# Holding back the gated delta rule's steps until a step of the other recurrence has run

## The chip, the core and the metric

The kernel runs on one NeuronCore of one Trainium2 chip. The metric is the device time of one execution in microseconds, and the runs shown are compared by their median. The core has five engines with a queue each: TensorE (PE in the profile, its weight loads PEld), VectorE (DVE), ScalarE (ACT), GpSimd (POOL) and SyncE (SP), which here issues all DMAs. An engine works through its queue in order and waits on semaphores for what other engines produce.

## The reference

One layer of a streaming encoder, for a prompt of 2048 tokens and for a sample of 8 requests of 16 tokens, with model width 1024. One projection feeds two recurrences, the gated delta rule (GDN, 4 heads of 128) and RWKV-7 (8 heads of 64). Their outputs are projected back and a convolutional feed-forward of width 2816 follows.

```python
h = rms_norm(x, norm_mix); p = h @ w_in              # 1024 x 3880
q, k, v, z, beta, log_g = ...                        # short convolution, silu, l2 norm, gates
S_t = g_t (I - b_t k_t k_t^T) S_{t-1} + b_t k_t v_t^T;  o_t = S_t^T q_t            # GDN, by blocks
R_t = R_{t-1} diag(w_t) + (R_{t-1} a_t) b_t^T + v_t k_t^T;  y_t = R_t r_t          # RWKV-7
x += concat(norm(o) * silu(z), (norm(y) + bonus) * g) @ w_out
up = rms_norm(x, norm_ffn) @ w_up                    # 1024 x 5632
x += (silu(causal_dwconv(up[:2816])) * up[2816:]) @ w_down
y = rms_norm(x, norm_final)                          # and all end states
```

## The kernel before, in words

**Tiling.** Channels lie on partitions, tokens along the free axis. The 16 prompt blocks of 128 tokens are cut into five groups of 3, 4, 3, 3 and 3 blocks; the last group also takes the sample's 128 tokens. A group's tile is 384 or 512 tokens wide.

**Projections.** Every weight block of 128 x 512 is loaded by SP into `w32` (4 buffers), rounded by ACT to `whi`, and the remainder `wlo` is made by POOL and DVE in turn (4 buffers of each). TensorE multiplies three times (`whi` with both halves of the activations, `wlo` with the rounded half) in `mm3`, which yields after every two of the eight tiles, that is after six products. The products' results are `psi` (input projection), `pso` (output projection), `psga` and `psup` (up), `psd` (down), in a PSUM pool of four banks.

**Recurrences.** Both work on blocks of 128 tokens by the same plan: products of keys and queries, the inverse of a unit triangular matrix by doubled blocks (seven levels, each a step with `pR` and a step with `pX`, in 16-bit floats), then `pP` and `pC` for one Newton step, then outputs and the new state in 32-bit floats. GDN (`gdn_block`, names with a g: `TUg`, `Nhg`, `gkq`) does four heads at once, so one chain of steps per block: `pE`, `pG`, `pd`, `pk` (decays, transposed keys), `pKK`, `pF`, the inverse, `pw`, `po` and `pS`. RWKV-7 (`rwkv_half`, names with an r: `TUr`, `Nhr`, `rX`) does four of its eight heads at once, so two chains per block: `pA` and `pT` twice, `pZ`, the inverse, `pSA`, `pY` and `pSr`. For the sample, GDN reads and writes its states by request in the small steps `pKS` and `pSs`. All recurrence products share a second PSUM pool of four banks, which DVE and ACT empty. A block's last step (the tails, `pt` for GDN and `ptr` for RWKV-7) follows 8 us later.

**What sets the order.** Each part is a Python generator that yields how long, in nanoseconds, its next products' operands will take. `drive` (L389) keeps a clock of TensorE's work as `mm` and `tr` estimate it, and writes TensorE's instructions one step after the other: of the tasks whose time has come it takes the one of the lowest rank number, and when none is due a step of the projections, the main chain. The ranks are 0 for the small parts of a projection, 1 for tails, 2 for RWKV-7, 3 for GDN. A step waits `lat` after its predecessor, 2200 ns in an input phase and 2400 ns in an output phase, or what it yields itself. TensorE is the only engine under `manual_schedule`; the other queues are ordered by the framework around it. The phases are three input projections ahead and then output and input phases by turns; an output phase begins when both recurrences of its group are done.

Of the kernel before, what the change touches and what calls it, by code (L numbers as in the profile page):

```python
# [39 lines left out]
LATO = 2400  # L40
NEPS = 1e-6
# [25 lines left out]
C_F32 = C_SI        # float32 up to here, masks behind  # L67
# [39 lines left out]
def pack_host(a):  # L107
    """Layout only: slices, transposes, zero padding."""
# [79 lines left out]
class Group:  # L188
# [6 lines left out]
    def seg(self, t):  # L195
        """the sample's part of a [p, tokens] AP, by request"""
        return t[:, self.P:self.n].rearrange("p (s t) -> p s t", t=SEG)


def bc(a, n):  # L200
    """a, along a new last axis"""
    return a.unsqueeze(len(a.shape)).to_broadcast(list(a.shape) + [n])


class Build:
# [7 lines left out]
    # ------------------------------------------------------------ set-up  # L213
    def setup(self, ctx):
# [11 lines left out]
        # what the first products need, before all else  # L226
# [37 lines left out]
        # constants by value  # L264
# [3 lines left out]
        # parameters worked out once  # L268
# [8 lines left out]
        self.cw = der("cw", q("cw"), 0.5, own=True)           # half the taps: silu(y) = (1 + tanh(y/2)) y/2  # L277
# [7 lines left out]
        self.nea = q("alog")                        # -exp(a_log)  # L285
        nc.scalar.activation(self.nea, q("alog"), AF.Exp)
        nc.vector.tensor_scalar(self.nea, self.nea, -1.0, None, op0=MUL)
        # the scan's resets
# [7 lines left out]
        # conv histories, and the sample's  # L296
# [12 lines left out]
        # per-token and per-block scalars  # L309
# [7 lines left out]
        # states: minus GDN's, and RWKV's with keys on partitions  # L317
# [4 lines left out]
        self.SB = [cp.tile([128, 2, 2, 64], F32, name=f"SB{i}") for i in range(2)]      # by pairs of heads, block-diagonal  # L322
# [3 lines left out]
        # scratch  # L326
        for i, g in enumerate(self.groups):
            d = lambda n, s: self.dp.tile(s, F32, name=f"{n}{i}")
            g.gd = d("gd", [4, 4, 128, g.n])        # k q v z, by head
            g.rx = [d(f"rx{j}_", [5, 128, g.n]) for j in range(4)]  # L330
            g.rh = d("rh", [8, 128, g.n])
            g.l2 = [d(f"l2{j}_", [6, g.n]) for j in range(4)]
            g.og = d("og", [8, 128, g.n])

    # ------------------------------------------------------------ small helpers
# [3 lines left out]
    def a(self, g, name, dt=F32):  # L339
        """of the ring that the feed-forward's activations have in their phase"""  # L340
        return self.tp_.tile([128, 532], dt, tag="act", name=name, bufs=NACT)[:, 0:g.n]
# [31 lines left out]
    # ------------------------------------------------------------ the order of TensorE's work  # L373
    # Every part is a generator that yields how long (ns) its next products' operands take; the
    # products of the projections fill the time between those of the recurrences.
# [13 lines left out]
    def drive(self, main):  # L389
        """main to its end, then what is left of the tasks"""  # L390
        main = [0.0, 0, main]
        while main[2] is not None or self.tasks:
            ready = [t for t in self.tasks if t[0] <= self.clock]
            if ready:
                self.step(min(ready, key=lambda t: (t[1], t[0])))
            elif main[2] is not None and main[0] <= self.clock:
                self.step(main)
            else:
                self.clock = min([t[0] for t in self.tasks] + ([main[0]] if main[2] is not None else []))
# [9 lines left out]
    def load_w(self, src, tiles=KT):  # L409
        """[128, tiles * 128] of a weight, by [128, 512]"""  # L410
# [8 lines left out]
    def split_w(self, src, tiles=KT, ws=None):  # L419
        """a weight as pairs of [128, 512]: rounded, and what is left"""  # L420
# [12 lines left out]
    def mm3(self, ps, w, xs):  # L433
        """ps = sum over tiles of w^T x, both split: three passes"""
# [10 lines left out]
    def load_tok(self, g, t, a):  # L445
        """a group's tokens from [128, all tokens] of DRAM"""
# [25 lines left out]
    def rms(self, g, acc):  # L472
        """in place: 1/rms of the channels whose squares acc sums by partition, on every partition"""
# [11 lines left out]
    def rsqrt(self, out, ps, scale=1.0):  # L485
        """(scale ps + eps)^-1/2"""
# [6 lines left out]
    def split_x(self, g, x, w=None):  # L493
        """x, times w of each channel: rounded, and what is left"""
# [10 lines left out]
    # ------------------------------------------------------------ causal convolution of a projected tile  # L505
    def conv(self, g, ps, rs, taps, hist, samp, out, rows=128):
        """out = conv of ps rs over the tokens; hist and samp become the last rows"""
# [28 lines left out]
    # ------------------------------------------------------------ input projection and all that is per token  # L536
    def phase_in(self, g):
# [17 lines left out]
        # low-rank inputs  # L555
# [29 lines left out]
    def gates(self, g, P, S):  # L585
        """beta and log decay of each token and GDN head, tokens on partitions"""
# [16 lines left out]
        # -beta = -(1 + tanh(b/2))/2  # L603
        nc.scalar.activation(w[0], ba[:, :, 0:4], AF.Tanh, scale=0.5)
        nc.vector.tensor_scalar(self.nbeta[:, sl], w[0], -0.5, -0.5, op0=MUL, op1=ADD)
        # log_g = -exp(a_log) (max(u,0) + ln(1 + exp(-|u|)))
# [9 lines left out]
    def l2scale(self, g, j, qk, kk):  # L616
        """(sum of squares over a head's channels + eps)^-1/2 of RWKV's keys, GDN's queries and keys: the sums
        side by side in the array, 32 rows each, and the results spread over the partitions through DRAM"""
# [47 lines left out]
    def prep_rwkv(self, g, j, block, la, sga, sgb, qk):  # L666
# [7 lines left out]
        # decay  # L674
# [12 lines left out]
        def pc(t):              # a tile's prompt tokens, by chunks  # L687
# [10 lines left out]
        # a chunk's exponents from its middle, the sample's from its start  # L698
# [16 lines left out]
        # learning rate a = (1 + th)/2  # L715
# [15 lines left out]
        def rest():  # L731
# [6 lines left out]
            # k (1 + (a - 1) k_a)  # L738
# [6 lines left out]
            # bonus and gate  # L745
# [14 lines left out]
            # the keys' direction  # L760
# [7 lines left out]
            # -kk a exp(-L)  # L768
# [8 lines left out]
    # ------------------------------------------------------------ inverse of four unit upper triangular matrices  # L777
    def inverse(self, N, levels, x):
        """(I - N)^-1 of N [128, 4, 128] (rows before columns): doubled blocks, then one Newton step"""
# [9 lines left out]
        for lv in range(levels):  # L789
# [3 lines left out]
            def v(t, o):        # [.., nb, b] of 128 columns: the first or the second of each pair of blocks  # L793
# [10 lines left out]
            if lv == 0:         # both from the identity, in which the products are plain  # L804
# [35 lines left out]
    # ------------------------------------------------------------ gated delta rule, a block of 128 tokens, four heads  # L840
    def gdn_block(self, g, i, samp=False):
# [11 lines left out]
        # decays  # L853
# [39 lines left out]
        # products of keys, queries with keys  # L893
# [11 lines left out]
        # through the state  # L905
# [50 lines left out]
        # norm over the head, gate  # L956
# [40 lines left out]
    # ------------------------------------------------------------ RWKV-7, a block of 128 tokens, four of the heads  # L997
    def rwkv_half(self, g, i, hf, samp=False):
# [21 lines left out]
        for p in range(2):  # L1020
            x = X[p]
            pA = [self.psr("pA").rearrange("p (n t) -> p n t", n=2) for e in range(2)]
            for n in range(2):
                for e in range(2):      # the halves of the array at once
# [49 lines left out]
        # outputs  # L1074
# [6 lines left out]
        # norm over the head, gate  # L1081
# [12 lines left out]
        # state  # L1094
# [59 lines left out]
    def rec(self, part):  # L1154
        """a recurrence through all groups, each once it is prepared"""
# [7 lines left out]
    # ------------------------------------------------------------ output projection and feed-forward  # L1163
# [75 lines left out]
    def finish(self, g, res, rs):  # L1239
        """the last norm"""  # L1240
# [34 lines left out]
def order(n):  # L1275
    """of the phases: three input projections ahead, then by turns"""
# [37 lines left out]
```

## Time and profile before

| | |
|---|---|
| median of 3 runs | 3566.49 us (3560.24 to 3572.14) |
| profiled execution, its span; the page gives no other time of it | 3558.0 us |
| TensorE busy | 3372.0 us, 95% |
| VectorE, GpSimd, ScalarE busy | 2376.5 us, 1833.0 us, 1510.7 us |
| mean granted TensorE clock | 0.972 |
| TensorE's weight loads busy | 2895.7 us |

The profiled execution's span is 8.5 us below the median of the runs and 2.2 us below the fastest. In a timeline row the first number is when the instruction, or the merged row, began, the second how long it lasted; rows of TensorE overlap, since its matmuls are pipelined, so what a product costs is the distance from its beginning to the next one's. A bracket gives the idle time of the engine before the row and who ended it. "L360" is the line of the helper `mm` that issues every product, so rows are told apart by their tiles.

### The profile page before, as it was taken

The page shows a single profiled execution, that of the slowest core. Times are in us where ns is not written, and L with a number is a line of the kernel's source. Part 1 is how long each engine was busy: PE and PEld are TensorE (multiplying, and loading weights), DVE is VectorE, ACT ScalarE, POOL GpSimd, SP SyncE. Part 2 cuts the span into 40 slices and gives each one's busy share as a digit, 9 for nine tenths or more (in the row PEclk, how much of TensorE's full clock was granted, in tenths as well). Part 3 has the DMA queues.
Part 4 walks back from the last instruction along what each step waited for, and adds up shares of the span by engine and source line. Part 5 has one row for each costly group of instructions (what it writes and reads, how often), then busy time and mean ns, then how long its engine had stood idle before and what let it go on. Part 6 is the DMA issues. An engine that isn't in the chain of part 4 may idle for free. (4 is left out here: it accounts for less than half of the span.)

```text
span 3558.0 us, 60074 instructions
## 1 busy us (share of the span) xinstructions
PE 3372.0 (95%) x21661; PEld 2895.7 (81%) x21661; DVE 2376.5 (67%) x4277; ACT 1510.7 (42%) x2698; POOL 1833.0 (52%) x2335
## 2 busy tenths in 40 slices
PE   8989989999999989999999999899999999999997
PEld 7867768788999977777777767799979899988886
DVE  7777777786776677666655677776566665665444
ACT  5554344444333455443333455443324434453333
POOL 4545545655664544455454445566555355534442
PEclk9989999999999999999999999999999999999999
DMA  5534444453333344532222334533343433443322
GB/s 174 167 130 131 140 150 128 139 167 107 110 108 114 123 140 143 169 97 86 92 92 92 112 136 143 191 112 112 112 140 121 159 123 129 137 139 97 97 94 81
DMA packets 346265, 447.58 MB, mean 126 GB/s; under 512 B 30168, under 2 KB 194336, under 8 KB 345968
## 3 DMA queue, kind: packets, MB, share of 16 engines
q1 hardware_dynamic: 345968, 443.75, 38.9%
q8 instruction: 170, 2.79, 0.3%
q14 instruction: 127, 1.04, 0.1%
HBM read 372.60 MB, written 71.03 MB: 125 GB/s over the span
## 5 line engine op out<-in xcount | busy, mean ns | idle before, releaser
L425 ACT CAST whi<-w 128x512 fp32r<-128x512 f32 (+1 forms) x1070 | 651.2, 610 | 1115.7 <-PE psd L360 295.5
L429 POOL TENSOR_TENSOR wlo<-w,whi 128x512 fp32r<-128x512 f32 (+1 forms) x535 | 706.9, 1321 | 676.3 <-ACT whi L425 625.2
L360 PE MATMUL psi<-x,whi 128*128 128x384 f32 (+1 forms) x2480 | 737.7, 378 | 33.8 <-ACT x L501 14.0
L360 PEld LDWEIGHTS psi<-x,whi 128*128 128x128 f32 x2480 | 456.4, 196 | 96.2 <-issue 23.9
L360 PE MATMUL psup<-x,whi 128*128 128x384 f32 (+1 forms) x1760 | 504.3, 367 | 0.0
L360 PE MATMUL psga<-x,whi 128*128 128x384 f32 (+1 forms) x1760 | 502.6, 366 | 0.0
L429 DVE TENSOR_TENSOR wlo<-w,whi 128x512 fp32r<-128x512 f32 (+1 forms) x535 | 426.2, 797 | 77.0 <-ACT whi L425 76.8
L360 PE MATMUL psi<-x,wlo 128*128 128x384 f32 (+1 forms) x1240 | 456.2, 368 | 3.2 <-POOL wlo L429 3.1
L360 PEld LDWEIGHTS psga<-x,whi 128*128 128x128 f32 x1760 | 315.5, 189 | 28.1 <-issue 3.3
L360 PEld LDWEIGHTS psup<-x,whi 128*128 128x128 f32 x1760 | 316.4, 190 | 25.7 <-issue 1.8
L360 PE MATMUL psd<-ah,whi 128*128 128x384 f32 (+1 forms) x880 | 330.2, 375 | 7.0 <-ACT ah L1213 7.0
L360 PE MATMUL psd<-al,whi 128*128 128x384 f32 (+1 forms) x880 | 319.7, 363 | 4.5 <-POOL al L1215 4.5
L360 PE MATMUL psd<-ah,wlo 128*128 128x384 f32 (+1 forms) x880 | 318.7, 362 | 0.0
L360 PE MATMUL psup<-x,wlo 128*128 128x384 f32 (+1 forms) x880 | 316.6, 360 | 0.0
L360 PE MATMUL psga<-x,wlo 128*128 128x384 f32 (+1 forms) x880 | 315.3, 358 | 0.0
L1223 DVE TENSOR_TENSOR res<-res,psd 128x384 f32<-128x384 f32 (+1 forms) x240 | 145.3, 605 | 212.8 <-PE psd L360 212.1
L360 PEld LDWEIGHTS psi<-x,wlo 128*128 128x128 f32 x1240 | 241.7, 195 | 26.3 <-POOL wlo L429 5.0
L1215 POOL TENSOR_TENSOR al<-xin,ah 128x384 fp32r<-128x384 f32 (+1 forms) x110 | 126.0, 1146 | 144.4 <-ACT ah L1213 100.7
L513 DVE TENSOR_TENSOR P<-psga,rsx 128x384 f32<-128x384 f32 (+1 forms) x110 | 64.2, 584 | 197.7 <-PE psga L360 192.5
L360 PE MATMUL pso<-x,whi 128*128 128x384 f32 (+1 forms) x640 | 187.5, 373 | 8.9 <-DVE x L499 7.4
L360 PEld LDWEIGHTS psd<-ah,whi 128*128 128x128 f32 x880 | 167.3, 190 | 23.9 <-ACT ah L1213 8.5
L821 DVE TENSOR_TENSOR TUr<-TUr,pX 128x256 f16<-128x256 f16 x396 | 148.5, 412 | 53.2 <-PE pX L360 51.7
(342 smaller groups left out, 6753.4 us busy)
## 6 DMA issues: line engine op xcount, KB each, us to landing
w<-in_w_up SPq DMA_DIRECT2D x440, 256.0 KB
w<-in_w_in SPq DMA_DIRECT2D x310, 256.0 KB
w<-in_w_down SPq DMA_DIRECT2D x160, 256.0 KB
rX<-rx SPq DMA_DIRECT2D x68, 320.0 KB
w<-in_w_out SPq DMA_DIRECT2D x80, 256.0 KB
w<-in_w_down SPq DMA_DIRECT2D x80, 192.0 KB
rx<-res SPq DMA_DIRECT2D x48, 192.0 KB
gd<-res SPq DMA_DIRECT2D x48, 192.0 KB
```

Of the source, the lines that this page charges most:

```text
L360: self.nc.tensor.matmul(out, lhsT=lhsT, rhs=rhs, start=start, stop=stop)
L425: nc.scalar.copy(hi, w)
L429: eng.tensor_tensor(lo, w, hi.bitcast(F32), SUB)
L513: nc.vector.tensor_tensor(P[:, h:h + g.P], ps[:, 0:g.P], rs[:, 0:g.P], MUL)
L821: nc.vector.tensor_tensor(w, w, pX[:, y].rearrange("p u (n b) -> p u n b", b=b), ADD)
L1215: nc.gpsimd.tensor_tensor(lo, y, hi.bitcast(F32), SUB)
L1223: nc.vector.tensor_tensor(res[m], res[m], ps, ADD)
```

## The change

`drive` holds a GDN step back. When a projection step could go and nothing but projection work has run since the last one (`joined` is false), tasks of rank 3 are left out of the choice, unless they have been due for `PATIENCE`, 3500 ns of the driver's clock. As soon as another task has put products in (a step of RWKV-7, a tail, a small part), `joined` becomes true and the GDN step that is due follows at once, ahead of the next projection step. Where no projection step can go, nothing is held back. The last branch now looks only at tasks whose time lies ahead. The rest of the diff takes out comments, which moves line numbers by one to eight.

```diff
+PATIENCE = 3500
...
     def drive(self, main):
         main = [0.0, 0, main]
+        joined = False
         while main[2] is not None or self.tasks:
             ready = [t for t in self.tasks if t[0] <= self.clock]
+            go = main[2] is not None and main[0] <= self.clock
+            if go and not joined:
+                ready = [t for t in ready if t[1] < 3 or t[0] + PATIENCE <= self.clock]
             if ready:
+                at = self.clock
                 self.step(min(ready, key=lambda t: (t[1], t[0])))
-            elif main[2] is not None and main[0] <= self.clock:
+                joined = joined or self.clock > at
+            elif go:
+                joined = False
                 self.step(main)
             else:
-                self.clock = min([t[0] for t in self.tasks] + ([main[0]] if main[2] is not None else []))
+                self.clock = min([t[0] for t in self.tasks if t[0] > self.clock] + ([main[0]] if main[2] is not None else []))
```

The instructions are the same in number and kind on every engine. Three places on TensorE show the move.

A step of GDN's inverse in the third group's output phase (`Nhg`, `TUg` are GDN's, `Nhr`, `TUr` RWKV-7's; `psga` and `psd` are projections). Before, a step alone:

```order
L360 MATMUL psga<-x,whi 128x384 x2
L360 MATMUL psga<-x,wlo 128x384
L360 LDWEIGHTS Nhg
L360 MATMUL pR<-TUg,Nhg 128x64
...
L360 MATMUL psga<-x,whi 128x384 x2
L360 MATMUL psga<-x,wlo 128x384
```

The same step with the change:

```order
L361 LDWEIGHTS nid_122
L361 MATMUL pP<-TUr,nid_122 128x128
L361 LDWEIGHTS Nhg
L361 MATMUL pR<-TUg,Nhg 128x64
...
L361 MATMUL psd<-ah,whi 128x384
L361 MATMUL psd<-al,whi 128x384
```

It stood between two projection steps; now it stands behind RWKV-7's `pP` step, with no projection product between the two. In the whole program TensorE leaves the projections 718 times before and 618 times with the change; of the 100 joints gained, 71 are between 16-bit steps of the two inverses.

The sample's state steps of GDN. Before, two of them with one projection step between:

```order
L360 MATMUL pSs<-gwm,gkt 128x512
L360 MATMUL psga<-x,whi 128x384 x2
L360 MATMUL psga<-x,wlo 128x384
L360 MATMUL psga<-x,whi 128x384 x2
L360 MATMUL psga<-x,wlo 128x384
L360 MATMUL pSs<-gwm,gkt 128x512
```

With the change, two of them in the same part:

```order
L361 MATMUL pR<-TUr,Nhr 128x64
L361 MATMUL pSs<-gwm,gkt 128x512
L361 MATMUL psd<-ah,whi 128x384
...
L361 MATMUL psga<-x,whi 128x384 x2
L361 MATMUL psga<-x,wlo 128x384
...
L361 MATMUL pR<-TUr,Nhr 128x64
L361 MATMUL pSs<-gwm,gkt 128x512
```

Each now follows a step of RWKV-7, and twelve projection products lie between the two where six lay.

The head of a GDN block in the third input phase. Before:

```order
L360 MATMUL pE<-lm,gtr 128x512 x2
L360 MATMUL pG<-lm,onr 128x512 x2
L360 MATMUL pd<-lg,con 128x4
L370 MATMUL pk<-con,gkq 128x128 x4
L360 LDWEIGHTS Nhr
L360 MATMUL pR<-TUr,Nhr 128x64
...
L360 MATMUL psi<-x,whi 128x384 x2
L360 MATMUL psi<-x,wlo 128x384
L370 MATMUL pt<-con,gon 128x128 x4
L360 MATMUL pKK<-gkq 128x256 x4
```

With the change:

```order
L361 MATMUL pE<-lm,gtr 128x512 x2
L361 MATMUL pG<-lm,onr 128x512 x2
L361 MATMUL pd<-lg,con 128x4
L371 MATMUL pk<-con,gkq 128x128 x4
L371 MATMUL pt<-con,gon 128x128 x4
L361 MATMUL pKK<-gkq 128x256 x4
L361 LDWEIGHTS TUr
L361 MATMUL pX<-Rr,TUr 128x64
```

The head's six tiles and the tail now come in one stretch, with no projection product inside it. Stretches that fill more than six banks before a projection product comes are 20 before and 32 with the change.

## The prediction

> **What bounds the kernel now.** I read the page first, then TensorE's waits, then its timeline at places where a recurrence step stands between projections.
>
> ```profile
> span 3558.0 us, 60074 instructions
> PE 3372.0 (95%) x21661; PEld 2895.7 (81%) x21661; DVE 2376.5 (67%) x4277; ACT 1510.7 (42%) x2698; POOL 1833.0 (52%) x2335
> PEclk9989999999999999999999999999999999999999
> ```
>
> TensorE bounds the whole span: 95% busy, the next engine 67%. So time can go in three ways only: TensorE's products take less each, it waits less (it is idle for 3558.0 - 3372.0 = 186.0 us), or its clock is granted more often. The third is in the view of cores:
>
> ```profile
> core 0: 3558.0 us, clock 0.972
> ```
>
> At a mean of 0.972 about 3558.0 x 0.028 = 100 us of the span went to a lower clock (an estimate, as if all of it were products). The waits, longest in total first, with their number and the longest one:
>
> ```profile
> PE pG L360 <- DVE rA L1027: 11.3, 2, 5.7
> PE pA L360 <- DVE rA L1027: 8.9, 5, 3.6
> PE pSs L360 <- DVE gwm L970: 7.3, 5, 2.9
> PE pR L360 <- DVE TUg L821: 3.3, 2, 2.7
> PE pKS L360 <- DMA gS<-in_st_gdn: 2.5, 1, 2.5
> PE pA L360 <- DVE SN L984: 2.1, 3, 0.7
> PE pX L360 <- DVE Rg L803: 1.6, 3, 0.7
> PE pE L360 <- POOL lm L857: 1.5, 2, 0.9
> PE pA L360 <- DVE gkt L890: 1.3, 1, 1.3
> ```
>
> The reader is to see two kinds. In five rows a GDN step waits for its own operands (`pSs` for `gwm`, `pR` for `TUg`, `pKS` for its state, `pX` for `Rg`, `pE` for `lm`): 7.3 + 3.3 + 2.5 + 1.6 + 1.5 = 16.2 us. In the other four, `pG` and `pA` wait for something that isn't their operand: DVE has not emptied the PSUM bank they want (11.3 + 8.9 + 2.1 + 1.3 = 23.6 us). The first kind shrinks when GDN comes later, the second can grow when recurrence steps stand closer.
>
> **The returns to the projections.** What a step costs beyond its products shows in TensorE's timeline. First a GDN step alone, as before the change; then one of the places where, already before, a GDN step happens to follow an RWKV-7 step of the same kind:
>
> ```profile
> 2387.41 0.51 PE L360 MATMUL psga<-x,whi 128*128 128x384 f32 x2
> 2387.76 0.34 PE L360 MATMUL psga<-x,wlo 128*128 128x384 f32 x1
> 2387.93 0.30 PE L360 MATMUL pR<-TUg,Nhg 128*128 128x64 f16 x4
> 2388.07 0.60 PE L360 MATMUL psga<-x,whi 128*128 128x384 f32 x2
> 2388.50 0.34 PE L360 MATMUL psga<-x,wlo 128*128 128x384 f32 x1
> ```
>
> ```profile
> 2402.44 0.33 PE L360 MATMUL psd<-ah,wlo 128*128 128x384 f32 x1
> 2402.61 0.29 PE L360 MATMUL pR<-TUr,Nhr 128*128 128x64 f16 x4
> 2402.74 0.28 PE L360 MATMUL pR<-TUg,Nhg 128*128 128x64 f16 x4
> 2402.85 0.42 PE L360 MATMUL psd<-ah,whi 128*128 128x384 f32 x1
> 2403.11 0.34 PE L360 MATMUL psd<-al,whi 128*128 128x384 f32 x1
> 2403.29 0.33 PE L360 MATMUL psd<-ah,wlo 128*128 128x384 f32 x1
> ```
>
> A projection product costs 0.175 us from beginning to beginning (2387.41 to 2387.76 for two). From 2387.76 to 2388.50 lie three products, 0.52 us, and the step: it costs 0.74 - 0.52 = 0.22 us. From 2402.44 to 2403.11 lie two products, 0.35 us, and two steps, which together cost 0.67 - 0.35 = 0.32 us. Apart they would cost 0.44. The saving is about 0.10 us a joint, with the rows' rounding 0.085 to 0.12; most of it is the first product behind a recurrence step, which takes 0.26 us (2402.85 to 2403.11) in place of 0.175.
>
> The order has 100 joints more. For the 71 between 16-bit steps I take the row: 71 x 0.10 = 7.1 us. For the other 29 a 32-bit step joins in, for which I quote no row of this kind; it can save nothing (the 32-bit step may pay the same start inside the stretch) or the same 0.10, and I take the middle, 29 x 0.05 = 1.5 us. The sum is **8.6 us**, with bounds 71 x 0.085 = 6.0 and 100 x 0.12 = 12.
>
> **GDN's own waits.** Held back, a step finds its operands more often. For `pSs` the order gives one more projection step, six products of 0.175 us or 1.05 us, between two of them. Five waits shortened by up to 1.05 us each are 5.2 us of the 7.3; the eight waits of the other four rows lose their whole length or 1.05 us each, 3.3 us to 1.65 for `TUg`, about 1.6 in `Rg`, 1.5 in `lm`, 1.05 in `pKS`: up to 5.8. Not all of it comes, since a step that starts later also makes its successor's operands later, and `PATIENCE` is counted on the driver's clock, which is not TensorE's own. I take half of the 11.0, rounded down: **5 us**; bounds 0 and 16.2.
>
> A held step also issues its DMAs later: a block's loads of `gkq` and `gV` with its first step, `gz` with `pw`, `gS` with `pKS` and `pSs`. They move with the step whose successors need them. SP's queue is not what they would hold up:
>
> ```profile
> SPq L415 <- POOL wlo L429: 1182.0, 450, 8.1
> SPq L415 <- DVE wlo L429: 714.6, 403, 7.0
> ```
>
> SP stands 1896.6 us waiting for a free weight buffer, so weights are loaded as early as buffers allow, and a GDN load that is issued a step later changes nothing ahead of it. I cost it at nothing; if a load came late it would appear as another row like that of `pKS`, 2.5 us.
>
> **PSUM banks.** Four banks serve both recurrences. What a bank wait looks like where a GDN head follows an RWKV-7 `pA`:
>
> ```profile
> 2286.89 1.28 DVE L1027 TENSOR_TENSOR rA<-pA,msk 128x512 f32<-128x512 f32 x2
> 2287.63 1.22 PE L360 MATMUL pG<-lm,onr 128*128 128x512 f32 x2 [5.56 <-DVE rA L1027]
> ```
>
> DVE needs 1.28 us for the two `rA`, but TensorE stood 5.56 us, because DVE came to them late. The change makes some of these places better (GDN's head no longer stands where it stood) and makes 12 more stretches of over six banks. On the one side, the two `pG` waits go, with 11.3 us, less what replaces them (I allow 3): -8 us. On the other, each of the 12 longer stretches waits for two evictions, 12 x 1.28 = +15 us. I take **0**, since the row stands for two places out of 17 heads, and keep both ends.
>
> **The clock.** It drops behind long waits:
>
> ```profile
> 2544.15 0.34 PE L360 MATMUL psga<-x,wlo 128*128 128x384 f32 x1
> 2547.04 1.05 PE L360 MATMUL pKS<-gkqs,gS 128*128 128x32 f32 x8 [2.55 <-DMA gS<-in_st_gdn]
> 2548.04 0.59 PE L360 MATMUL psga<-x,whi 128*128 128x384 f32 x2
> 2552.03 0.52 PE L360 MATMUL psup<-x,wlo 128*128 128x384 f32 x1
> ```
>
> After 2.55 us without a product the same product shows 0.52 us in place of 0.34. Over the kernel, 100 us lost to the clock stand beside 186.0 us of idle time, 0.54 for each. For the 5 us of waits saved that is **2.7 us**. The Trainium skill, in "TensorE: Matmul & The Clock Gate", section "HAM oscillation — how this bites in real kernels", has the clock fall to half when an idle gap crosses a window of about 3.4 us, and not in proportion to all idle time. By that rule short waits that shrink bring back no clock at all and the sum would be 2.7 us less. The row above agrees as to its kind, with a gap of 2.55 us.
>
> **The sum.** 8.6 + 5 + 0 + 2.7 = 16.3 us, from 3558.0 to about 3542 us of span. The median shown lies 8.5 us over the span; I carry that along: 3566.5 - 16.3 = 3550 us. All favourable bounds together are 12 + 16.2 + 8 + 0.54 x 24.2 = 49 us; all unfavourable, 15 + 0.54 x 15 - 6.0 = 17 us slower.
>
> **Rivals.** *Only the returns.* Waits move rather than vanish: the waits that a later GDN step avoids come back at RWKV-7's `pA`, which now finds GDN's tiles ahead of it. Then 8.6 us are left: 3558 us, which counts as no change. For it speaks that GDN's own waits are only 16.2 of 186.0 us of idle time; against it, that RWKV-7 keeps the first place whenever both are due.
>
> *The banks turn the sign.* In the head shown in the order, `pE`, `pG`, `pd`, `pk`, `pt`, `pKK` and RWKV-7's `pX` come with no projection product between. If each of the 12 added stretches waits for the 1.28 us of two evictions and GDN's own waits don't shrink, that is 15.4 us, and 0.54 of it again from the clock, 23.7 in all; less 8.6 from the returns it is 15 us slower, 3582 us. It decides from 8.6 / (12 x 1.54) = 0.47 us a stretch. For it speak the 23.6 us of bank waits; against it, that 20 such stretches already stand in the program and only the few rows above came of them. The Trainium skill, in "Perfetto Trace Analysis", section "Optimizing Tensor Performance", asks that independent groups of matmuls rotate through banks so that emptying one overlaps with the next group's products; this change takes away the projection products that did that here.
>
> *GDN becomes the last.* If it fell behind RWKV-7, an output phase would wait for it.
>
> ```profile
> L360 PE MATMUL pS<-gw,gkt x128: 274/275/276, 299.7 to 2525.3; 128*128 128x128 f32 x128
> L360 PE MATMUL pSr<-rSA,rtok x256: 221/222/271, 290.1 to 2759.1; 128*64 128x64 f32 x128
> ```
>
> GDN's last prompt block ends 234 us ahead of RWKV-7's. A block has some 22 steps; at 3.5 us each the last group's three blocks and its sample lose 308 us, 74 too many: 3640 us. But that needs every step held to the limit, though RWKV-7 has a step about every 3 us.
>
> **How the numbers follow.** I give the forecast 0.53, only the returns 0.26, the banks 0.19, the late GDN 0.02. What counts as a change is 0.3%, 10.7 us, about what a measurement of this kernel can tell. The first case is faster, the second the same (with a hundredth more for cases near the bound), the others slower with a hundredth off: 0.53, 0.27, 0.20. The range reaches down by 38 us, not the full 49, since all favourable bounds will hardly meet, and up to the bank rival: 3528 to 3581 us. The likeliest case alone spans 3536 to 3556.
>
> **What would show it.** Right: more places where `pR<-TUg` follows `pR<-TUr` or `pX` without a projection product; the waits `pSs <- gwm`, `pR <- TUg` and `pX <- Rg` smaller in sum than 13; a mean clock of 0.972 or a little more. The return's price is wrong if the joined steps cost 0.44 together. The bank term is wrong if waits of `pG`, `pA`, `pKK` or `pX` for a DVE row that isn't their operand sum to well over 23.6 us. The whole is wrong if idle time grows, which would mean that waits on DVE, busiest in the input phases, follow another pattern than the rows quoted here.

## The result, and the profile after

| | before | with the change |
|---|---|---|
| median of 12 runs each | 3563.24 us (3559.36 to 3572.14) | 3543.36 us (3532.66 to 3562.39) |
| ratio | | 0.9947, 95% interval 0.9935 to 0.9959 |
| profiled execution: its own time; its span | not given; 3558.0 us | 3551.17 us; 3549.3 us |
| mean granted TensorE clock, median of the runs | 0.973 | 0.977 |

The change is faster by 19.9 us, 0.53%; by the interval 15 to 23 us. The forecast was 16.3 us faster. The sign and the size came as predicted. The terms did not all hold, and most of what follows is about that.

The page and the cores view of the changed kernel, to be held against the first rows of the prediction:

```profile
span 3549.3 us, 60010 instructions
PE 3360.1 (95%) x21661; PEld 2893.1 (82%) x21661; DVE 2396.0 (68%) x4277; ACT 1512.3 (43%) x2698; POOL 1837.8 (52%) x2335
```

```profile
core 0: 3549.3 us, clock 0.975
```

TensorE is busy for 3372.0 - 3360.1 = 11.9 us less, and idle for 189.2 us, not 186.0: this pair shows no gain in waits. Two cautions belong to these numbers. The profiled execution of the change lies above the median of its runs (3551 against 3543), so it shows 8.7 us of the 20. The profile before was one of the faster runs: a run of the change takes 1.9 us longer than its span, and the prediction carried 8.5. And two profiles of the kernel before differ by 6 us in TensorE's busy time (3372.0 and 3365.8) and 9 us in its idle time (186.0 and 194.7), so differences of that size in one pair prove nothing.

The waits of TensorE in the changed kernel (total us, number, longest), first GDN's own and the banks, then three rows of RWKV-7:

```profile
PE pSs L361 <- DVE gwm L978: 6.9, 2, 4.5
PE pX L361 <- DVE Rg L811: 6.0, 3, 4.6
PE pR L361 <- DVE TUg L814: 2.6, 3, 1.1
PE pR L361 <- DVE TUg L829: 2.4, 4, 1.2
PE pE L361 <- POOL lm L865: 0.4, 1, 0.4
PE pA L361 <- DVE rA L1035: 23.1, 11, 5.4
PE pA L361 <- DVE gkt L898: 0.9, 1, 0.9
...
PE pX L361 <- DVE Rr L811: 14.2, 11, 4.6
PE pR L361 <- DVE TUr L829: 11.6, 10, 3.6
PE pZ L361 <- DVE rA L1035: 1.4, 3, 1.1
```

The rows of RWKV-7 that answer to these in the kernel before, which the prediction did not show:

```profile
PE pZ L360 <- DVE rA L1027: 8.0, 3, 4.1
PE pR L360 <- DVE TUr L806: 6.1, 2, 5.9
PE pX L360 <- DVE Rr L803: 5.6, 5, 3.9
PE pR L360 <- DVE TUr L821: 4.3, 6, 1.2
```

The reader is to see that waits changed place. The two `pG` waits on `rA` (11.3 us) and the `pKS` wait on its state (2.5) are gone. But `pA` on `rA` went from 8.9 to 23.1, `pX` on `Rr` from 5.6 to 14.2, and `pR` on `TUr` from 10.4 to 12.1 (11.6 and, by the same view, 0.5 at L814); `pZ` on `rA` fell from 8.0 to 1.4. Summed over all rows of the two views, the waits in front of GDN's steps fell from 38.6 to 24.1 us, and those in front of RWKV-7's rose from 63.6 to 78.8.

The joined step, in the timeline, behind `pP` where the order showed it:

```profile
2407.45 0.22 PE L361 MATMUL pP<-TUr,nid 128*128 128x128 f16 x1
2407.50 0.28 PE L361 MATMUL pR<-TUg,Nhg 128*128 128x64 f16 x4
2407.62 0.42 PE L361 MATMUL psd<-ah,whi 128*128 128x384 f32 x1
2407.88 0.34 PE L361 MATMUL psd<-al,whi 128*128 128x384 f32 x1
```

`pR` takes 0.12 us to the next product, and the 0.26 us of the first projection product is paid once for both steps: the price that the prediction read from the kernel before. It is no matter of one place: in the profile before, the first 384-wide projection product behind a 16-bit step took 0.259 us in the median of 326 places at full clock, one behind another projection product 0.174. Two long stretches show that one without a projection product can go with or without a wait. A head in an output phase, seven tiles and no wait:

```profile
2392.77 0.29 PE L361 MATMUL pR<-TUr,Nhr 128*128 128x64 f16 x4
2392.90 0.70 PE L361 MATMUL pE<-lm,gtr 128*128 128x512 f32 x2
...
2394.95 1.89 PE L361 MATMUL pKK<-gkq 128*128 128x256 f32 x8
2396.68 0.28 PE L361 MATMUL pX<-Rr,TUr 128*128 128x64 f16 x4
```

And a stretch where an input phase ends and an output phase begins:

```profile
770.54 0.29 PE L361 MATMUL pR<-TUg,Nhg 128*128 128x64 f16 x4
770.76 1.13 PE L361 MATMUL pA<-rX 64*128 64x256 f32 x8
...
777.00 0.37 PE L361 MATMUL pX<-Rg,TUg 128*128 128x64 f16 x4 [4.62 <-DVE Rg L811]
779.61 2.07 PE L361 MATMUL pA<-rX 64*128 64x256 f32 x6 [0.88 <-DVE rA L1035]
782.95 0.52 PE L361 MATMUL pso<-x,wlo 128*128 128x384 f32 x1
```

Here GDN's `pX` holds everything for 4.62 us, though its `pR` had been through 6 us before, because DVE made `Rg` late; then `pA` waits for a bank, and the projection behind shows 0.52 us instead of 0.34. This need not be a price of the change: near the same change of phase the kernel before stands too, 4.07 us at `pZ` for `rA`.

### The profile page after: what moved, and what is told of

Its sections match the earlier page's. It is cut to its first block, busy times and chain, and to the rows that moved or that the text cites. A ratio compares the mean times of both kernels' runs of the same rounds, so it can differ in the third digit from the quotient of the medians.

```text
span 3549.3 us, 60010 instructions
## 1 busy us (share of the span) xinstructions
PE 3360.1 (95%) x21661; PEld 2893.1 (82%) x21661; DVE 2396.0 (68%) x4277; ACT 1512.3 (43%) x2698; POOL 1837.8 (52%) x2335
## 5 line engine op out<-in xcount | busy, mean ns | idle before, releaser
L437 DVE TENSOR_TENSOR wlo<-w,whi 128x512 fp32r<-128x512 f32 (+1 forms) x535 | 435.3, 814 | 77.0 <-ACT whi L433 76.1
```

What stands on the lines that cost most here:

```text
L437: eng.tensor_tensor(lo, w, hi.bitcast(F32), SUB)
```

## The experiments

Three properties of an order can be told apart: how late a GDN step goes after it is due (its mean in the driver's own order), how often TensorE leaves the projections ("returns", counted in the order), and which steps meet which work of DVE. The theories on trial are those of the prediction (the returns; GDN's own waits; the banks; the clock) and, from the second kernel on, a rival: that a later GDN step is what helps, joined or not.

| kernel | returns | GDN late by, us | median us | ratio to before, 95% | median clock |
|---|---|---|---|---|---|
| before, again | 718 | 1.10 | 3563.36 | 1.0000 (0.9987 to 1.0012) | 0.973 |
| the change | 618 | 1.46 | 3543.36 | 0.9947 (0.9935 to 0.9959) | 0.977 |
| held, never joined | 925 | 1.59 | 3564.11 | 0.9998 (0.9986 to 1.0011) | 0.9755 |
| joined early, not held | 638 | 0.73 | 3603.52 | 1.0118 (1.0099 to 1.0138) | 0.9665 |
| held, and joined early | 619 | 1.08 | 3552.99 | 0.9980 (0.9964 to 0.9995) | 0.9755 |
| later, not joined | 737 | 1.35 | 3542.58 | 0.9944 (0.9923 to 0.9965) | 0.978 |
| inverse steps only | 630 | 1.32 | 3560.50 | 0.9993 (0.9976 to 1.0009) | 0.972 |
| other steps only | 683 | 1.18 | 3554.43 | 0.9977 (0.9962 to 0.9993) | 0.976 |
| the change, both recurrences later | 643 | | 3537.91 | 0.9930 (0.9910 to 0.9951) | 0.977 |
| another order (parts) | 717 | 1.02 | 3563.87 | 1.0002 (0.9993 to 1.0012) | 0.976 |
| another order (tails) | 717 | 1.10 | 3555.71 | 0.9981 (0.9972 to 0.9990) | 0.975 |
| sample steps only | 709 | 1.16 | 3557.44 | 0.9982 (0.9970 to 0.9994) | 0.974 |
| the change, GDN later | 626 | 1.96 | 3556.93 | 0.9977 (0.9968 to 0.9986) | 0.974 |

(Lateness counts the 400 ns where an experiment adds them; it is left out where both recurrences were moved.)

**The kernel before again**, unchanged, as a measure of what a comparison can tell.

> The kernel before, unchanged, for the span and the granted clock of each of its runs. Theory 'clock': its clock lies near 0.970 to 0.972 where the changed kernel's twelve runs had 0.972 to 0.981 with a median of 0.977, and over the runs of both kernels span falls by about 3.3 us for each 0.001 of clock, so that at one and the same clock the two kernels differ by less than 5 us. Theory 'returns': the clocks of both kernels are alike, and at one clock the changed kernel is 8 us or more faster.

Measured: 3563.36 us beside 3563.66, ratio 1.0000 within 0.0012. A difference of 5 us between two kernels is visible here; whether it belongs to the edit is another question, taken up below. The median clock was 0.973 (0.971 to 0.977), the change's 0.977, so the clocks are not alike; at one clock the change is some 8 to 10 us faster by the medians, and neither theory described both.

**Held, never joined.** A GDN step still waits for another step, but one projection step is put between.

```diff
-        joined = False
+        joined = 0
...
-            if go and not joined:
+            if go and joined != 2:
...
-                joined = joined or self.clock > at
+                joined = 1 if self.clock > at else joined
             elif go:
-                joined = False
+                joined = 2 if joined == 1 else 0
```

> GDN's steps are held back as in the change, but a held step goes only after one projection step has followed the other task's step, so that it never follows that step at once. TensorE leaves the projections 925 times (718 before, 618 with the change); GDN's steps start 1.59 us after they are due on the driver's clock (1.10 before, 1.46 with the change). Theory 'returns' (each costs 0.085 to 0.10 us): 207 more than before, 18 to 21 us slower than before, about 3583 us. Theory 'later steps' (what gains is that GDN's operands have more time): as late as with the change or later, so the gain of the waits stays, 3545 to 3555 us if returns cost nothing, about 3565 us with returns at 0.10.

Measured: 3564.11 us, as before, with 207 returns more. Against the change these are 307 returns and 20.8 us, 0.07 us each, at about the same lateness and a clock lower by 0.0015. If lateness were worth nothing, 207 returns at 0.10 us would have made it 21 us slower, and 12 at the 0.06 us found below.

**Joined early, not held.** Nothing waits; behind another step a GDN step that is due within 1000 ns goes at once.

```diff
-PATIENCE = 3500
+EARLY = 1000
...
-            if go and not joined:
-                ready = [t for t in ready if t[1] < 3 or t[0] + PATIENCE <= self.clock]
+            if joined and not ready and self.clock != tried:
+                tried = self.clock
+                ready = [t for t in self.tasks if t[1] == 3 and t[0] <= self.clock + EARLY]
```

> Nothing is held back; instead, behind a step of another task, a GDN step that falls due within the next 1.0 us of the driver's clock goes at once. TensorE leaves the projections 638 times (718 before, 618 with the change), but GDN's steps start 0.73 us after they are due, earlier than before (1.10). Theory 'returns': 80 returns less at 0.085 to 0.10 us, 7 to 8 us faster than before, about 3556 us. Theory 'later steps': GDN's operands have less time than before, waits grow, slower than before, 3570 us or more. Theory 'clock': the time follows the granted clock, 3.3 us for each 0.001, whichever way that goes.

Measured: 3603.52 us, 40 us slower than before, with 80 returns fewer. The page, and the waits that grew:

```profile
PE 3383.7 (94%) x21661; PEld 2904.9 (81%) x21661; DVE 2386.7 (66%) x4277; ACT 1510.5 (42%) x2698; POOL 1836.6 (51%) x2335
```

```profile
PE pSs L361 <- DVE gwm L979: 11.2, 6, 4.2
...
PE pKS L361 <- DMA gS<-in_st_gdn: 5.1, 1, 5.1
```

`pSs` waits 11.2 us where it waited 7.3, `pKS` 5.1 where it waited 2.5, and all GDN steps together 64.1 where they waited 38.6. TensorE is idle for 3601.9 - 3383.7 = 218.2 us, 32 us more, and busy for 11.7 us more at a clock of 0.966. Fewer returns alone therefore do not make the kernel faster; a GDN step that goes ahead of its operands costs more than the return it saves.

**Held, and joined early.** The change, and behind another step also GDN steps due within 600 ns (the branch above, added to the change with `EARLY = 600`).

> The change, and besides, behind a step of another task, a GDN step that falls due within the next 0.6 us goes at once. TensorE leaves the projections 619 times, as with the change (618); GDN's steps start 1.08 us after they are due, as before (1.10). Theory 'returns': as fast as the change, 3543 us within 5. Theory 'later steps': the gain from waits is lost again and only that of the returns stays, about 3555 us.

Measured: 3552.99 us. The lateness is back at 1.08 us with the returns of the change, and half of the gain is gone, as theory 'later steps' had it; the half is 9.6 us between two orders, little more than the 7.5 us that another order is worth below.

**Later, not joined.** The kernel before, with each GDN step due 400 ns later. Nothing waits for another step.

```diff
+LATE = 400
...
-            task[0] = self.clock + (next(task[2]) or 0)
+            at, ns = self.clock, next(task[2]) or 0
+            task[0] = at + ns + (LATE if task[1] == 3 and ns > 500 else 0)
```

> The kernel before, but every GDN step is due 0.4 us later on the driver's clock; nothing is held for another task's step and nothing is joined. GDN's steps then start 0.95 us after that later time, 1.35 us after the old one (1.10 before, 1.46 with the change). TensorE leaves the projections 737 times (718 before, 618 with the change). Theory 'later steps': GDN's own waits fall from about 35 us to about 23, as with the change; less 19 returns at 0.10 us, the time is 3553 to 3558 us. Theory 'returns': 2 us slower than before, about 3565 us. Theory 'only the joint': lateness without joining gains nothing, 3563 us.

Measured: 3542.58 us, all that the change brings, with 19 returns more than before. So a gain of this size needs no joint. But the mechanism of theory 'later steps' did not come: it expected GDN's own waits to fall by 12 us, and the waits in front of GDN's steps sum to 40.6 us, where they were 38.6 before. Its page line and waits:

```profile
PE 3350.8 (95%) x21661; PEld 2871.7 (81%) x21661; DVE 2384.0 (67%) x4277; ACT 1509.3 (43%) x2698; POOL 1829.3 (52%) x2335
```

```profile
PE pX L361 <- DVE Rr L805: 21.6, 15, 3.5
PE pG L361 <- DVE rA L1029: 9.7, 2, 6.1
PE pA L361 <- DVE rA L1029: 3.5, 3, 1.9
```

Idle time is 3537.4 - 3350.8 = 186.6 us, against 186.0 and 194.7 in the two profiles of the kernel before. Busy time is 21.2 us less than in the first of them and 15.0 less than in the second, with products of the same number and kind at a clock of 0.980 in place of 0.972 and 0.974. So most of the gain is in busy time, and it may all be. `pA` waits 3.5 us for banks, where the change has 23.1.

How much the same idle time can leave of the clock shows in three of the waits of the kernel before between 1000 and 1800 us, in TensorE's timeline, and then in stretches of 14 us around them (the number behind POOL's is the granted clock):

```profile
1328.27 0.37 PE L360 MATMUL pX<-Rr,TUr 128*128 128x64 f16 x4 [3.91 <-DVE Rr L803]
1368.37 1.19 PE L360 MATMUL pZ<-rtok,rA 128*128 128x64 f32 x4 [3.51 <-DVE rA L1027]
1469.18 0.79 PE L360 MATMUL pso<-x,whi 128*128 128x512 f32 x1 [5.04 <-DVE x L499]
```

```profile
1324.00:1338.00 14.00, 10.09 (x59) 8.96 (x58) 13.32 (x25) 5.05 (x10) 5.63 (x9) 0.76 0.62 201
1365.00:1379.00 14.00, 10.63 (x52) 10.16 (x53) 9.76 (x17) 4.61 (x8) 6.47 (x8) 0.76 0.59 197
1461.00:1475.00 14.00, 7.70 (x21) 4.64 (x22) 9.83 (x19) 6.22 (x12) 1.78 (x2) 0.63 0.75 249
```

The same two views of the kernel with later GDN steps:

```profile
1287.89 0.28 PE L361 MATMUL pX<-Rr,TUr 128*128 128x64 f16 x4 [2.09 <-DVE Rr L805]
1372.52 0.28 PE L361 MATMUL pX<-Rr,TUr 128*128 128x64 f16 x4 [3.54 <-DVE Rr L805]
1412.76 0.28 PE L361 MATMUL pX<-Rr,TUr 128*128 128x64 f16 x4 [2.46 <-DVE Rr L805]
```

```profile
1286.00:1300.00 14.00, 12.11 (x81) 11.79 (x80) 12.67 (x20) 6.89 (x13) 7.05 (x13) 0.88 0.27 91
1370.00:1384.00 14.00, 11.48 (x73) 10.51 (x73) 13.41 (x24) 5.02 (x10) 6.33 (x8) 0.88 0.51 169
1411.00:1425.00 14.00, 11.74 (x84) 11.13 (x84) 13.79 (x26) 4.74 (x9) 5.86 (x9) 1.00 0.74 246
```

The trace also records from when to when the clock was granted by half: in stretches of 3.41 us or whole multiples of it. A granted clock of 0.76 over 14 us is two such stretches, 0.63 three and 0.88 one. So the waits of 3.91 us (half clock from 1326.57 to 1333.39) and 3.51 us go with two each, the 3.54 and the 2.09 with one, the 2.46 with none. At the 5.04 us there are three, but they begin at 1463.10, a microsecond before that wait, behind two shorter waits. Half clock costs only while TensorE has products, and some of it lies inside the waits. Half of the rest is lost: 2.6, 3.0 and 2.6 us in the three places before; 1.7, 1.7 and 0 in the three here (estimates from these records).

Over the profile, half clock is 200 us before (183 in the other profile of that kernel) and 143 here. TensorE was busy in 155 (138) and 110 us of it, and half of the difference, 14 to 22 us, is most or all of the gain. Waits of more than 3 us number 14 (15) before and 11 here.

**The change for a part of the steps**: the inverse alone, all but the inverse, and the sample block alone. `self.gin` is set around the call of the inverse in `gdn_block`, `self.gsamp` at the sample block in `rec_gdn`. The line is shown for the inverse alone; for all but the inverse it has `or self.gin`, for the sample `or not self.gsamp`.

```diff
-                ready = [t for t in ready if t[1] < 3 or t[0] + PATIENCE <= self.clock]
+                ready = [t for t in ready if t[1] < 3 or not self.gin or t[0] + PATIENCE <= self.clock]
```

> The change for the steps of GDN's inverse alone (pR, pX, pP, pC and the pw behind them); the other GDN steps go as before. TensorE leaves the projections 630 times, 88 of the 100 returns that the change saves. Theory 'returns': 88 x 0.086 = 7.6 us and their share of the clock, 3548 to 3556 us. Theory 'later steps': the inverse's own waits are the smaller part (pR and pX, 9 of 35 us), so 3 to 5 us for them besides, 3550 us; where all that the change gives comes with these steps, 3543 us.

> The change for the GDN steps outside its inverse alone (the block's head, pKK, pF, po, pS, and the sample's pKS and pSs). TensorE leaves the projections 683 times, 35 less than before. Theory 'returns': 35 x 0.086 = 3 us, 3560 us. Theory 'later steps': the longer waits lie here (pG 11.3, pSs 7.3, pKK 3.5, pKS 2.5 us), so half of the change's gain or more, 3550 to 3555 us.

> The change for GDN's sample block alone (its pKS and pSs among it). TensorE leaves the projections 709 times, 9 less than before. If what the steps outside the inverse gave (3554 us) comes from the sample's state steps, where the 17 us at half clock stood, 3554 us. If it comes from the heads of the prompt blocks, 3562 us.

Measured, against the before run beside each: inverse -3.5 us, the others -9.6 us, the sample -5.7 us. The inverse has 88 of the 100 joints and its interval holds zero, with the median clock at 0.972; brought to one clock by the slope over the runs (2.5 to 3.3 us for each 0.001), it is 4 to 7 us faster, 0.05 to 0.08 us a return. None of the times expected for the inverse came; the other steps came as theory 'later steps' had them, and the sample lies between its two times. The inverse also counts against lateness as the cause: its GDN steps are 1.32 us late, as in the kernel of later steps (1.35), with 107 returns fewer, and the 20 us are not there. Inverse and others together make 13.1 us, not 20, but each of the two is uncertain by some 6 us, so this does not tell whether the parts add up.

**The change, with both recurrences later.** `LATI` from 2200 to 2500, `LATO` from 2400 to 2700.

> The change, and both recurrences' steps get 0.3 us more for their operands (2500 and 2700 ns in place of 2200 and 2400). TensorE leaves the projections 643 times (618 with the change): 25 x 0.09 = 2 us more. RWKV-7 ends 95 us later on the driver's clock, still 120 us ahead of the last output phase. Theory 'later steps' extended to RWKV-7: its waits for DVE (about 148 of 171 us are not GDN's) fall by a tenth or more and the clock rises with them: 3520 to 3535 us, faster than the change. Theory 'returns': 3545 us, a little slower than the change. If the waits are set by DVE's backlog of several us and not by the tenths of a microsecond, nothing moves: 3545 us.

Measured: 3537.91 us (3534.76 to 3544.01). It beats both kernels in its median, by 5.5 us over the change; the intervals of the two ratios overlap, and the next two runs say what 5 us between two orders are worth. The time lies between the two that were expected.

**Other orders.** The kernel before with numbers moved that have nothing to do with GDN's steps: the parts of a projection 400 ns later (`LB` and `LC` 12400 for 12000), and in another kernel the tails 300 ns later (`LT` 8300 for 8000).

> The kernel before with another order that has nothing to do with GDN's lateness: the small parts of an input projection (psl, psbo, psgt) come 0.4 us later. TensorE leaves the projections 717 times (718 before), GDN's steps start 1.02 us after they are due (1.10). Theories 'returns' and 'later steps': no change, 3563 us within 4. Theory 'any other order' (what moved the time is that waits fall differently in any new order): it moves by 8 us or more, either way.

> As the run with later small parts, but the tails (pt and ptr) come 0.3 us later: TensorE leaves the projections 717 times, GDN's steps start 1.10 us after they are due. Theories 'returns' and 'later steps': no change, 3563 us within 4. Theory 'any other order': it moves by 8 us or more, either way.

Measured: +0.7 us, and -7.5 us with an interval clear of zero. A new order can be worth 7.5 us for no reason that one could name beforehand. So differences of 5 to 8 us between two orders (the parts of the change, or later steps for both against the change) do not stand out. The 20 us of the change and of the later steps, and the 40 us of the early ones, do against these two; two orders do not say how far a third could go. The first of the two also has a median clock of 0.976 and only 8 waits of over 3 us without any gain: over different orders neither is by itself a shorter time.

**The change, with GDN later still** (the `LATE` edit on top of the change).

> The change, and GDN's steps are due 0.4 us later besides. TensorE leaves the projections 626 times, 111 less than in the run that was only later (737, 3542.6 us). If the returns and the lateness add up, 111 x 0.07 to 0.10 = 8 to 11 us less than that: 3531 to 3535 us. If the joint gives nothing once GDN is late, 3543 us. If GDN is now later than its waits can use, 3543 us as well, and its own waits are no smaller than with the change.

Measured: 3556.93 us, 6 us faster than before and 14 us slower than either edit alone, which none of the theories had. The two do not add. The row that grew:

```profile
PE pA L362 <- DVE rA L1037: 35.9, 18, 6.1
```

`pA` waits for banks: 8.9 us before, 3.5 with later steps alone, 23.1 with the change, 35.9 with both. It is not the joint as such that costs this: the inverse alone has 88 returns fewer and `pA` at 8.2 us, early joining 80 fewer and 7.5, while the other steps alone have 35 fewer and 17.5. So the row grows where the steps outside the inverse, the heads among them, are held and joined. Nor does lateness help by itself: this is the latest of the kernels, and the waits in front of its GDN steps are the shortest of all, 15.2 us, but RWKV-7's are 91.5.

**Where the time went, by profile.** TensorE's busy time can be split by the clock records: half of what it was busy at half clock is lost to the clock, and the rest is what its products would take at full clock (an estimate; us).

| profile | returns | products at full clock | lost to the clock | idle |
|---|---|---|---|---|
| before; before, again | 718 | 3294.5; 3296.9 | 77.4; 68.9 | 186.0; 194.7 |
| the change | 618 | 3287.1 | 73.0 | 189.2 |
| held, never joined | 925 | 3306.9 | 67.6 | 187.8 |
| joined early, not held | 638 | 3290.4 | 93.4 | 218.2 |
| later, not joined | 737 | 3295.9 | 54.9 | 186.6 |
| the change, GDN later | 626 | 3286.9 | 78.3 | 190.6 |

The first column of times goes with the returns: a straight line through all fourteen profiles has 0.06 us a return (standard error 0.01). The other two do not go with returns or lateness alone.

## Why the prediction was right, and where it was not

**The returns (8.6 us): upheld, at the low end of its bounds.** The joined step shows the same 0.12 and 0.26 us. The prediction took 0.10, between the 0.12 by which its two rows differ (0.44 and 0.32) and the 0.085 of the first product. Over fourteen orders a return is worth 0.06 us of products, so 100 of them 6 us; in the profiles the change's products at full clock take 7.4 and 9.8 us less than in the two before. By the medians of runs, the two kernels closest in lateness give 0.07 us a return (the change against held, never joined), and later and not joined against held and never joined 0.11, but that pair lies 0.0025 apart in clock. The 32-bit steps, for which the prediction quoted no row, show the same first product, 0.260 us in the median of 83 places. Early joining, with 80 returns fewer and 40 us more, shows that this term decides only as long as no step is moved ahead of its operands.

**GDN's own waits (-5 us): failed.** The step was "Held back, a step finds its operands more often". The five rows were 16.2 us; they are 6.9 + 6.0 + 2.6 + 2.4 + 0.4 = 18.3 now, 2 us more where 5 less were forecast. The prediction's own mark, `pSs`, `pR` and `pX` below 13 us in sum, stands at 17.9. `pKS` did lose its wait and `pSs` waits twice in place of five times, but once for 4.5 us, and `pX` waits 4.62 us for `Rg`. The five rows were a choice, though. All waits in front of GDN's steps did fall, by 14.5 us, most of it at `pG`'s banks (11.3); but those in front of RWKV-7's rose by 15.2, so nothing came of it. A step's place behind another one does not say where DVE is in its queue, and DVE makes most of these operands.

**The banks (0): upheld as a sum.** The four rows were 23.6 us; `pA` on `rA` and `gkt` now make 24.0. The `pG` waits went, with 11.3 us, and `pA` took 14.2 more, close to the 15 us that the rival had asked for. The gain of one bound and the loss of the other both came, and that they cancel is luck as much as judgement: the prediction took 0 as a middle.

**The clock (2.7 us): mis-sized.** The term was "0.54 for each" us of idle time saved. No idle time was saved in the profile, and the median clock over the runs rose by 0.004. At 2.5 us for each 0.001 (the kernel before, over its runs) to 3.1 (the change) that is 10 to 12 us. What is left of the 20 is 8 to 10 us, in which the returns have room. The change's one profile does not show these 10 to 12 us: 73.0 us are lost to the clock there, between the 77.4 and 68.9 of the two before; it is one of the slower runs. The 100 us from which the 0.54 came are 77 by the clock records, since part of the half clock falls into waits. And the clock is not lost in proportion to idle time: in the rows above it is 3.0 us for 3.51 us of waiting, 1.7 for 3.54 and for 2.09, nothing for 2.46. The Trainium skill's rule, in "TensorE: Matmul & The Clock Gate", section "HAM oscillation — how this bites in real kernels", that the clock falls when a gap crosses a window of about 3.4 us, fits five of the six rows, but neither the 2.09 us here nor the prediction's own row of 2.55 us. All fourteen profiles together say more. Take the waits that stand alone: no half clock and under 0.3 us of other waits in the 7 us before, no other wait over 0.5 us in the 3.5 us behind, the first 25 and the last 45 us of a run left out. Half clock began during the wait or in the 3.5 us behind it in 13 of 94 waits of 1 to 1.75 us, 81 of 103 of 2 to 3 us, 35 of 40 of 3 to 3.41 us, and 86 of 87 longer ones. So a wait over 3.4 us nearly always goes with half clock, as the rule has it, but most of 2 to 3 us do as well. The prediction drew from that rule only that short waits bring nothing back; it also asks which waits are long, and that was not followed.

So the forecast was right by its first term and by two misses that nearly offset each other, which is luck: own waits 7 us too favourable, the clock 7 to 9 us too small. Its own sign that the whole is wrong, idle time that grows, is not decided: 189.2 us stand against 186.0 and 194.7. Of the rivals, *only the returns* described the waits correctly (they move rather than vanish: 102.2 us in front of both recurrences' steps before, 102.9 after) and missed the clock. *The banks turn the sign* had the right place and price in `pA`, and not the gain at `pG` beside it. GDN did not become the last:

```profile
L361 PE MATMUL pS<-gw,gkt x128: 275/275/275, 305.6 to 2559.4; 128*128 128x128 f32 x128
L361 PE MATMUL pSr<-rSA,rtok x256: 222/222/271, 290.4 to 2724.9; 128*64 128x64 f32 x128
```

It ends 165 us ahead of RWKV-7, 68 us less than before.

**What is shown and what stays open.** Shown: a return costs 0.06 to 0.085 us, so the change saves 6 to 8.5 us by them; with the change waits move from GDN's steps to RWKV-7's and their sum stays; one kernel with later GDN steps and no joint is as fast, mostly by less half clock and not by shorter GDN waits; steps ahead of their operands lose 40 us. For the rest of the change's gain the clock over its runs speaks, and which of its waits cost less clock stays open: the profile, above the median of the runs, has 15 waits of over 3 us where the two before have 14 and 15. That lateness is the cause is not shown. The inverse alone (1.32 us late, 630 returns) and the change with GDN later (1.96 us, 626) have what both theories ask for, and gain 3.5 and 6 us. Why one order has waits that cost the clock less than another is not known. What such a wait is made of can be seen on DVE in the kernel before, ahead of the 3.91 us above:

```profile
1323.20 0.62 DVE L764 SCALAR_TENSOR_TENSOR gth<-rk,par,res 128x384 f32<-128x384 f32 x1 [4.60 <-DMA res<-l]
...
1325.32 2.08 DVE L637 SCALAR_TENSOR_TENSOR res<-res 128x384 f32<-128x384 f32 x2
1327.33 0.55 DVE L769 SCALAR_TENSOR_TENSOR gth<-ra,gth 128x384 f32<-128x384 f32 x1
1327.80 0.41 DVE L803 TENSOR_TENSOR Rr<-pR,msk 128x256 f16<-128x256 f32 x1
```

DVE stood 4.60 us for a DMA, then worked off what was queued, and `Rr` came last. GDN has no part in this piece. Which step of which recurrence is caught by such a stand depends on the order, and that may be how an order without any better idea behind it came out 7.5 us better; no run shows it.

## What to carry to other kernels

Where one engine takes steps from several chains of dependences in a fixed order, ask first whether the steps go too early: moving them ahead of their operands cost 40 us here. A delay costs one number to try (0.4 us brought as much as the joining here, once), but it is no rule: with the joining on top it took most of the gain away. Pack short steps together for the price of a return (0.06 to 0.085 us each here) only where the banks they fill are emptied in time, and sum the waits of both chains before a shorter wait in one of them is called a gain. Before a gain of a few tenths of a per cent is put down to an idea, run the same program with an order that differs for no reason.

## What was not expected of the hardware

- One program without any change of its work takes 3532.66 to 3562.39 us, and the granted clock goes with it: 3530.8 us of span at 0.981, 3560.5 at 0.972. One profile can lie anywhere in that, so the clock of several runs belongs beside every comparison of two profiles.
- Nearly the same idle time of TensorE (186.0, 194.7 and 186.6 us) goes with 77, 69 and 55 us lost to the clock. How idle time is cut into waits matters beside its sum, but not by their length alone: waits of 3.51 and 3.54 us went with 3.0 and 1.7 us, and 22 of the 103 lone waits of 2 to 3 us with nothing.
- The first projection product behind any recurrence step, 16-bit or 32-bit, takes 0.26 us in place of 0.174 at full clock, in 326 and 83 places of one profile.
